# Differential attention: rotation of the heads split over ScalarE and one GpSimd multiply, softmax left undivided, output scaled on ScalarE

## The chip, the cores and the metric

The kernel runs on one core of a Trainium2 chip. The metric is the device time in microseconds of one execution, as the median of several runs. Five engines work side by side, each through its own list of instructions in order: TensorE (PE; its weight loads are PEld), VectorE (DVE), ScalarE (ACT), GpSimd (POOL) and SyncE (SP), which only starts transfers here. An instruction that waits holds up all that stand behind it on its engine.

## The reference, cut to what matters

A small network on 256 tokens of width 1024: a first block of two layers, then a second block of two. Each layer has a mixer, an attention to a memory and a feed-forward, each with a layer norm. The change touches the mixer of the first block's second layer, a differential attention with 8 heads of 2 x 64:

```python
def rope(t):
    ...
    t1, t2 = tf[..., : d // 2], tf[..., d // 2:]
    return jnp.concatenate([t1 * cos - t2 * sin, t1 * sin + t2 * cos], axis=-1).astype(t.dtype)

def block(qi):
    s = jnp.einsum('bqhcd,bkhcd->bhcqk', qi, k).astype(jnp.float32) * scale
    p = jax.nn.softmax(s, axis=-1)
    a = p[:, :, 0] - lam * p[:, :, 1]
    return jnp.einsum('bhqk,bkhe->bqhe', a.astype(v.dtype), v)

o = diff_attention(q, k, v, lam)
o = rms_norm(o, subln_g) * (1.0 - lam_init)
return o.reshape(B_, S, C_WIDTH) @ w_out
```

Queries and keys are rotated, two softmaxes of a head are subtracted with a factor `lam`, the values are weighted with the difference, and the result of each head is divided by its root mean square (with `LN_EPS` under the root).

## The kernel before, in words

All products are made in float32 precision from two parts: each weight tile `w` of 128x1024 is loaded by SyncE's queue, rounded by ScalarE to `wh` (L218), and the rest is formed by VectorE as `wl` (L219). TensorE then multiplies three times (L348, L350, L352 for products with features on the partitions; L307 to L309 in `mm3`). Four tiles can be on their way (`STAGE`), and ten pairs can lie ready (`W_SLOTS`).

There is no scheduler. The order of each engine's list is the order in which the Python code issues instructions. Heads are generators in `self.bgs`: each call of `tick` (after a projection of 128 features, `unit_group`) moves every live head to its next `yield`, and the table `PACE` says how many ticks a head rests at its points d0 to d7. So several heads are under way at once, each at another stage.

For head `h`, `odd` projects queries and keys to one PSUM bank `ps` of 128x512 (two `unit_a`), ScalarE copies it to `oqk` (L1099), and the generator `head` goes on:

- d0: GpSimd multiplies four quarters of 32 partitions by the sine table, each into the quarter beside it of `qr` (L1041); VectorE multiplies `oqk` by the cosine (L1042);
- d1: VectorE adds both to `qr` (L1044);
- d2: TensorE forms the scores of both halves of the head (L1051), VectorE their row maxima (L619, L623);
- d3: ScalarE takes the exponentials with their sums (L627, four instructions);
- d4: VectorE divides the first softmax (L631, L635 twice), takes the reciprocal of the second sum times minus `lam` (L631, L1067) and blends both (L1069 twice);
- d5: TensorE transposes the blend (L644), ScalarE copies it to `pT` (L646);
- d6: TensorE multiplies with the values (L1078), ScalarE sums the squares (L1083), VectorE adds the epsilon (L1084), GpSimd raises to the power -1/2 (L522), VectorE scales the output `oz` (L1087);
- d7: TensorE transposes it (L1091), ScalarE and VectorE split it into two parts (L295, L296).

In the middle of the stage one turn of TensorE's list is: values of head h, scores of head h+2, a half projection of head h+5, transposed output of head h, transposed blend of head h+1, the other half projection. After the last head, products of the memory's keys (`mem_fill`) take the place of the projections.

Of the kernel before, what the change touches and what calls it, by code (L numbers as in the profile page):

```python
# [15 lines left out]
S = 256  # L16
# [11 lines left out]
# ---------------------------------------------------------------- host layout  # L28


def blk_a(w):
    """[K, N] -> [N/128, 128, K] : one unit holds 128 output columns."""
    k, n = w.shape
    return w.reshape(k // 128, 128, n // 128, 128).transpose(2, 1, 0, 3).reshape(n // 128, 128, k)


def blk_v(w, ck, cols):
    """[K, N] -> [N/cols * K/128/ck, 128, ck*cols] : moving weights, ck row tiles by cols columns."""
    k, n = w.shape
    u = k // 128 // ck  # L40
    return (w.reshape(u, ck, 128, n // cols, cols).transpose(3, 0, 2, 1, 4)
            .reshape(n // cols * u, 128, ck * cols))
# [6 lines left out]
def blk_t(x):  # L49
    """[256, 1024] -> transposed [2, 128, 4*256] (two units of four feature tiles)."""  # L50
    return x.T.reshape(2, 4, 128, S).transpose(0, 2, 1, 3).reshape(2, 128, 4 * S)
# [10 lines left out]
def constants():  # L62
    i = np.arange(128)
    row, col = i[:, None], i[None, :]
    c = {}
    ident = (row == col).astype(np.float32)
    negt = np.where(row >= col, -1, 0).astype(np.float32)
    strict = (row < col).astype(np.float32)
    c["c_sq"] = np.stack([ident, negt, strict], 1).copy()
    ncn = np.zeros((128, 384), np.float32)  # L70
    ncn[:, 0:128] = np.where(col > row, -BIG, 0)
    ncn[:, 256:384] = ncn[:, 0:128]
    c["c_ncn"] = ncn
    cc = np.arange(64)
    start = np.clip(cc - 8, 0, 48)
    win = (cc[None, :] >= start[:, None]) & (cc[None, :] < start[:, None] + 16)
    na = np.where(win, 0, -BIG).astype(np.float32)
    c["c_na"] = np.tile(na[:, ::-1], (2, 6)).reshape(128, 6, 64).copy()
    inv = (np.float32(10000.0) ** (-np.arange(0, 64, 2, dtype=np.float32) / np.float32(64)))
    ang = (np.arange(S, dtype=np.float32)[:, None] * inv[None, :]).astype(np.float32)  # L80
    cos = np.tile(np.cos(ang).T.astype(np.float32), (4, 1))
    sin = np.sin(ang).T.astype(np.float32)
    sin = np.tile(np.concatenate([sin, -sin], 0), (2, 1))
    c["c_rope"] = np.stack([cos, sin], 1).copy()
    oh = np.zeros((32, 512), np.float32)
    oh[t5_buckets(), S - 1 + np.arange(S)] = 1.0
    c["c_t5"] = oh
    return c
# [79 lines left out]
# ---------------------------------------------------------------- device  # L168


class Blank:
    """Stands for every object while the order of the weights is recorded."""
# [17 lines left out]
class Stream:  # L190
    """Weights in the order of their use: loaded ahead, split into two float32r parts ahead."""
# [75 lines left out]
class Net:  # L267
# [8 lines left out]
    # ---- small helpers  # L276
# [27 lines left out]
    def mm3(self, ps, a, b, first, last):  # L304
        """ps (+)= (a0+a1)^T (b0+b1) without the product of the two low parts below float32's rounding."""
        mm = self.nc.tensor.matmul
        mm(ps, a[0], b[0], start=first, stop=False)  # L307
        mm(ps, a[0], b[1], start=False, stop=False)  # L308
        mm(ps, a[1], b[0], start=False, stop=last)  # L309
# [18 lines left out]
    def flush(self, n=99):  # L328
        """Emit up to n pieces of the layer norm that is still due."""
        while self.pending and n:  # L330
            try:
                next(self.pending[0])
            except StopIteration:
                self.pending.pop(0)
                self.ws.more(3)
            n -= 1

    # ---- projections
    def unit_group(self, units):
        """units: (ps, name, index) - 128 output features of x @ W each, feature-major, row tiles outermost."""  # L340
# [16 lines left out]
    def unit_a(self, ps, name, idx):  # L357
        """128 output features of x @ W, feature-major, into ps [128, 256]."""
        self.unit_group([(ps, name, idx)])

    def vproj(self, name, groups, evac):
        """x @ W token-major, 512 columns a group."""
# [22 lines left out]
    def vproj_first(self, name, evac):  # L385
        """The first product: each row tile as soon as it and its weights are there."""
# [16 lines left out]
    # ---- output projection, residual and layer norm  # L403
# [108 lines left out]
    def ln_r(self, t, n, c):  # L512
        """x <- c x + the columns of the output projection; their statistics."""
        nc = self.nc
        lo, hi = self.COLS[t][n]
        r = self.x[:, t, lo:hi]
        nc.vector.scalar_tensor_tensor(r, in0=r, scalar=c, in1=self.acc[t][n], op0=OP.mult, op1=OP.add)
        nc.vector.bn_stats(self.st[t][:, n, :], r)
# [27 lines left out]
    def ln_t(self, t, lo, hi):  # L546
        """Columns lo:hi of x, transposed, as two parts."""
# [7 lines left out]
    # ---- feed-forward  # L555
    def ffn(self, pre, li, c, eps, hold=6):
# [10 lines left out]
        # the first two tiles of hidden features token-major: the first tokens' part does not wait for the others  # L567
# [43 lines left out]
    # ---- softmax along the free dimension  # L611
    def softmax(self, s, src, widths, scale=1.0, norm=True):
        """s <- softmax(scale * src) for the blocks of a [128, sum(widths)]; src may be PSUM."""
# [11 lines left out]
        for i in range(n):  # L625
            w = slice(off[i], off[i] + widths[i])
            nc.scalar.activation(s[:, w], src[:, w], AF.Exp, scale=scale, bias=mx[:, i:i + 1],  # L627
                                 accum_out=sm[:, i:i + 1])
        yield
        r = self.col(n)  # L630
        nc.vector.reciprocal(r, sm)  # L631
        if norm:
            for i in range(n):
                w = slice(off[i], off[i] + widths[i])
                nc.vector.tensor_scalar(s[:, w], s[:, w], r[:, i:i + 1], None, op0=OP.mult)  # L635
        self.sm_r = r

    def transpose_p(self, s):
        """s [128 t, 2 (t), 256 s] -> [128 s, 2 (s), 256 t]."""
# [9 lines left out]
    # ---- attention to the memory  # L649
    def mem_open(self, pre, mem, kd):  # L650
        """The memory's keys and values do not depend on x: jobs that fill gaps."""
# [118 lines left out]
    # ---- layer 0 of the first block  # L770
    def even(self):
# [11 lines left out]
        def na_load(p):  # L783
            if p < 4:
                nbs[p] = [self.k2([128, 6, 64], name="bt") for _ in range(2)]
                for e, bt in enumerate(nbs[p]):
                    # rows of keys relative to the first row of the query's half, from -2; columns reversed
# [65 lines left out]
        # gates, as rows: heads of the forward direction from 0, of the backward one from 32  # L853
# [65 lines left out]
        def lstm_head(h, y):  # L919
# [13 lines left out]
            for d in range(2):  # L933
# [6 lines left out]
                # columns of E: forward (s0: t0 t1, s1: t1), backward (s0: t0, s1: t0 t1)  # L940
# [78 lines left out]
    # ---- layer 1 of the first block  # L1019
    def odd(self):  # L1020
# [4 lines left out]
        cos = rp[:, 0:1, :].to_broadcast([128, 2, S])  # L1025
# [10 lines left out]
        def head(h, qk):  # L1036
            yield from self.pause("d0")
            qr = self.k2(name="qr")
            for b in range(4):
                i, o = slice(32 * b, 32 * b + 32), slice(32 * (b ^ 1), 32 * (b ^ 1) + 32)  # L1040
                nc.gpsimd.tensor_mul(qr[o], qk[i], rp[i, 1:2, :].to_broadcast([32, 2, S]))  # L1041
            nc.vector.tensor_mul(qk, qk, cos)  # L1042
# [3 lines left out]
            ss, gs, rs = [], [], []  # L1046
            for c in range(2):
                rows = slice(64 * c, 64 * c + 64)
                ps = self.bank()
                for tt in range(2):  # L1050
# [4 lines left out]
                                 scale=0.125, norm=c == 0)  # L1055
# [3 lines left out]
            yield from self.pause("d3")  # L1059
            for g in gs:  # L1060
                next(g)
            yield from self.pause("d4")
            for g in gs:
                for _ in g:
                    pass
                rs.append(self.sm_r)
            nc.vector.tensor_scalar(rs[1], rs[1], nlam, None, op0=OP.mult)  # L1067
            for tt in range(2):
                nc.vector.scalar_tensor_tensor(ss[0][:, tt, :], in0=ss[1][:, tt, :], scalar=rs[1][:, tt:tt + 1],  # L1069
                                               in1=ss[0][:, tt, :], op0=OP.mult, op1=OP.add)  # L1070
            yield from self.pause("d5")
# [12 lines left out]
            nc.vector.tensor_scalar(q, q, 1.0 / 128, EPS, op0=OP.mult, op1=OP.add)  # L1084
            y = self.rsqrt(q, 2)
            for tt in range(2):
                nc.vector.tensor_scalar(z[:, tt, :], po[:, tt, :], y[:, tt:tt + 1], None, op0=OP.mult)  # L1087
# [6 lines left out]
        for h in range(8):  # L1094
# [3 lines left out]
            qk = self.k2(name="oqk")  # L1098
            nc.scalar.copy(qk, ps)  # L1099
            self.bgs.append(head(h, qk))  # L1100
# [4 lines left out]
    # ---- mixer of the second block  # L1105
    def mixer(self, l, li):
# [85 lines left out]
        # index scores  # L1192
# [47 lines left out]
        # the 64 largest scores of a row, lower index first among equals, as an additive mask  # L1240
# [20 lines left out]
        # the shared latent key / value  # L1261
# [4 lines left out]
        def latent():  # L1266
# [18 lines left out]
            # keys of each head's queries: the latent keys through its up-projection  # L1285
# [13 lines left out]
        # short convolution  # L1299
# [119 lines left out]
    def rel_table(self):  # L1419
        """Rows of rel_bias by distance, one for each head, to DRAM."""  # L1420
# [10 lines left out]
    def rel_rows(self, t, h):  # L1431
        """Bias of the causal blocks for each query, keys from the last to the first: distance i at 255 + i."""
# [28 lines left out]
    def tables(self):  # L1461
        nc, sg, nlam, lp = self.nc, self.sg, self.nlam, self.lp
        nc.vector.tensor_scalar(sg, sg, 1.0 - LAM_INIT, None, op0=OP.mult)
        # lambda, negated, on every partition
# [119 lines left out]
```

## Time and profile before

| | |
|---|---|
| median of 3 runs | 2338.8 us (2338.48 to 2339.41) |
| profiled execution, first to last instruction | 2336.7 us |
| busy: PE, PEld, DVE, ACT, POOL | 98%, 92%, 66%, 49%, 10% of the span |
| mean granted clock of TensorE | 0.993 of full |
| chain that ended last | PE 91%, DVE 3%, issue 2%, DMA 1%, POOL 1%, ACT 1% |
| the changed stage | about 480 to 612 us |

How to read it: the page gives no second time of the profiled execution besides its span; the runs were timed apart, and their median is 2.1 us longer than the span. A busy share is a mean over all stages. The chain is followed back from the last instruction, at each step to what released it. In the timeline a row is a start, a duration, the engine, the line of the kernel, the operation, what it writes and reads, a count, and in brackets the idle time before it with what ended it.

### The profile page before, as it was taken

How to read it: one execution, taken by the hardware profiler on the slowest of the kernel's cores; microseconds unless marked ns; L12 is line 12 of the kernel's file. 1: busy time of each engine (PE TensorE's matmuls, PEld its weight loads, DVE VectorE, ACT ScalarE, POOL GpSimd, SP SyncE). 2: the span in 40 equal slices, each digit the busy share in tenths (PEclk: the TensorE clock that was granted, in tenths of full speed). 3: DMA queues.
4: the chain of work that ended last, by engine and by line, in shares of the span. 5: the costliest groups of instructions: out<-in, count | busy, mean ns of one | idle time of the engine just before them, and what ended most of it. 6: DMA issues, size and time to landing. Idle time of an engine off the chain costs nothing.

```text
span 2336.7 us, 41017 instructions
## 1 busy us (share of the span) xinstructions
PE 2281.4 (98%) x16600; PEld 2142.5 (92%) x16600; DVE 1533.1 (66%) x2303; ACT 1138.5 (49%) x1816; POOL 241.5 (10%) x263
## 2 busy tenths in 40 slices
PE   7999999977999999999999999999999999999998
PEld 6889999977899999999999999999999999999998
DVE  5885665678757657656487677656656577677655
ACT  5555454344454444543844554443543745545542
POOL 0720000044100000000202100000000101200000
PEclk9999999998999999999999999999999999999999
DMA  7645476352355664754455555753764446454752
GB/s 236 155 163 172 162 243 189 122 192 88 128 189 181 216 189 137 242 182 136 163 154 165 170 184 184 235 184 126 253 189 155 145 142 182 156 193 165 249 186 74
DMA packets 118080, 407.50 MB, mean 174 GB/s; under 512 B 14169, under 2 KB 19418, under 8 KB 117890
## 3 DMA queue, kind: packets, MB, share of 16 engines
q1 hardware_dynamic: 116258, 402.00, 52.9%
q0 software_dynamic: 768, 1.57, 0.8%
q8 instruction: 130, 2.13, 0.4%
q10 hardware_dynamic: 864, 1.31, 0.2%
q14 instruction: 60, 0.49, 0.1%
HBM read 403.76 MB, written 1.06 MB: 173 GB/s over the span
## 4 chain that ended last, share of the span: by engine, by line
PE 91%; DVE 3%; issue 2%; DMA 1%; POOL 1%; ACT 1%; ACTq 0%; DVEq 0%; POOLq 0%; SPq 0%
PE ps L348 16%; PE ps L350 16%; PE ps L352 16%; PE acc L307 7%; PE acc L308 7%; PE acc L309 7%; PE ps L307 5%; PE ps L309 4%; PE ps L308 4%; PE ps L725 1%; PE ps L745 1%; PE ps L551 1%; PE ps L644 1%; POOL qr L1041 1%; DMA xq<-in_xT 1%
## 5 line engine op out<-in xcount | busy, mean ns | idle before, releaser
L219 DVE TENSOR_TENSOR wl<-w,wh 128x1024 fp32r<-128x1024 f32 x725 | 888.5, 1245 | 360.8 <-ACT wh L218 357.6
L348 PE MATMUL ps<-xT,wh 128*128 128x256 f32 x3232 | 924.2, 286 | 0.0
L350 PE MATMUL ps<-xT,wl 128*128 128x256 f32 x3232 | 916.9, 284 | 0.0
L352 PE MATMUL ps<-xT,wh 128*128 128x256 f32 x3232 | 916.4, 284 | 0.0
L218 ACT CAST wh<-w 128x1024 fp32r<-128x1024 f32 x725 | 748.2, 1050 | 234.5 <-PE ps L352 135.4
L348 PEld LDWEIGHTS ps<-xT,wh 128*128 128x128 f32 x3232 | 622.5, 193 | 10.0 <-issue 5.5
L350 PEld LDWEIGHTS ps<-xT,wl 128*128 128x128 f32 x3232 | 622.6, 193 | 0.6
L352 PEld LDWEIGHTS ps<-xT,wh 128*128 128x128 f32 x3232 | 622.3, 193 | 0.0
L307 PE MATMUL acc<-wh,ph 128*128 128x512 f32 (+1 forms) x940 | 329.2, 350 | 0.6 <-ACT ph L295 0.6
L308 PE MATMUL acc<-wl,ph 128*128 128x512 f32 (+1 forms) x940 | 327.2, 348 | 0.0
L309 PE MATMUL acc<-wh,pl 128*128 128x512 f32 (+1 forms) x940 | 325.9, 347 | 0.0
L307 PEld LDWEIGHTS acc<-wh,ph 128*128 128x128 f32 x940 | 177.9, 189 | 24.9 <-ACT ph L295 0.8
L309 PEld LDWEIGHTS acc<-wh,pl 128*128 128x128 f32 x940 | 177.5, 189 | 23.2 <-DVE pl L296 0.2
L308 PEld LDWEIGHTS acc<-wl,ph 128*128 128x128 f32 x940 | 178.0, 189 | 22.3
L522 POOL TENSOR_TENSOR col<-col,mhalf 128x1 f32<-128x1 f32 (+1 forms) x38 | 28.6, 753 | 1610.1 <-DVE col L530 1469.7
L563 ACT ACTIVATE k<-ps 128x256 f32<-128x256 f32 x120 | 46.0, 383 | 178.3 <-PE ps L352 178.3
L307 PE MATMUL ps<-wh 128*128 128x256 f32 x384 | 113.3, 295 | 0.0
L292 ACT CAST ph<-k 128x256 fp32r<-128x256 f32 x120 | 48.8, 407 | 129.7 <-DVE k L565 129.7
L564 DVE SCALAR_TENSOR_TENSOR k<-k,ps 128x256 f32<-128x256 f32 x120 | 50.4, 420 | 93.4 <-ACT k L563 93.2
L307 PE MATMUL ps<-wh,xT 128*128 128x256 f32 (+1 forms) x304 | 102.2, 336 | 8.5 <-ACT wh L218 8.4
L309 PE MATMUL ps<-wh,wl 128*128 128x256 f32 x384 | 109.3, 285 | 0.0
L308 PE MATMUL ps<-wl,wh 128*128 128x256 f32 x384 | 109.2, 284 | 0.0
(264 smaller groups left out, 2548.1 us busy)
## 6 DMA issues: line engine op xcount, KB each, us to landing
w<-in_h_g SPq DMA_DIRECT2D x160, 512.0 KB, 4.4
w<-in_h_d SPq DMA_DIRECT2D x88, 512.0 KB, 4.3
w<-in_f_g SPq DMA_DIRECT2D x80, 512.0 KB, 4.3
w<-in_m_gate SPq DMA_DIRECT2D x48, 512.0 KB, 4.2
w<-in_f_d SPq DMA_DIRECT2D x44, 512.0 KB, 4.1
gb<-in_ln_row SPq DMA_DIRECT2D x28, 512.0 KB, 6.5
w<-in_m_c SPq DMA_DIRECT2D x24, 512.0 KB, 3.3
w<-in_m_br SPq DMA_DIRECT2D x24, 512.0 KB, 3.5
```

The lines of the kernel that those rows point to most:

```text
L218: n.nc.scalar.copy(hi[:, :cols], w[:, :cols])
L219: self.due = lambda: n.nc.vector.tensor_sub(lo[:, :cols], w[:, :cols], hi[:, :cols].bitcast(F32))
L292: nc.scalar.copy(hi, src)
L307: mm(ps, a[0], b[0], start=first, stop=False)
L308: mm(ps, a[0], b[1], start=False, stop=False)
L309: mm(ps, a[1], b[0], start=False, stop=last)
L348: mm(ps, ws[i][0][:, k, :], xh[:, k, :], start=k == 0, stop=False)
L350: mm(ps, ws[i][1][:, k, :], xh[:, k, :], start=False, stop=False)
L352: mm(ps, ws[i][0][:, k, :], xl[:, k, :], start=False, stop=k == 7)
L522: self.nc.gpsimd.tensor_tensor(y, v, self.mhalf[:, :n], op=OP.pow)
L563: nc.scalar.activation(h, pg, AF.Tanh, scale=0.5)
L564: nc.vector.scalar_tensor_tensor(h, in0=h, scalar=1.0, in1=pg, op0=OP.add, op1=OP.mult)
```

## The change

ScalarE no longer copies `ps` to `oqk` whole: it copies its four quarters of 32 partitions, each to the neighbouring quarter of `qr`. GpSimd then multiplies all of `qr` by the sine in place, one instruction a head (the table's signs are exchanged for it). VectorE takes the cosine product straight from `ps`. The first softmax is not divided: with row sums s0 and s1, the blend is e0 - lam (s0 / s1) e1, which is s0 times the wanted difference; the epsilon under the root is multiplied by s0 squared, so that the root mean square takes the factor out again. The output is scaled by ScalarE. Lines behind the softmax shift by one to five, so the same instruction has another line number in the changed kernel.

```diff
-    sin = np.tile(np.concatenate([sin, -sin], 0), (2, 1))
+    sin = np.tile(np.concatenate([-sin, sin], 0), (2, 1))
...
+        self.sm_s = sm
         yield
+        if norm is None:
+            return
         r = self.col(n)
         nc.vector.reciprocal(r, sm)
...
-        def head(h, qk):
+        def head(h, qk, qr):
             yield from self.pause("d0")
-            qr = self.k2(name="qr")
-            for b in range(4):
-                i, o = slice(32 * b, 32 * b + 32), slice(32 * (b ^ 1), 32 * (b ^ 1) + 32)
-                nc.gpsimd.tensor_mul(qr[o], qk[i], rp[i, 1:2, :].to_broadcast([32, 2, S]))
-            nc.vector.tensor_mul(qk, qk, cos)
+            nc.gpsimd.tensor_mul(qr, qr, sin)
             yield from self.pause("d1")
             nc.vector.tensor_add(qr, qr, qk)
...
-                                 scale=0.125, norm=c == 0)
+                                 scale=0.125, norm=None)
...
+            sums = []
             for g in gs:
                 next(g)
+                sums.append(self.sm_s)
             yield from self.pause("d4")
-            for g in gs:
-                for _ in g:
-                    pass
-                rs.append(self.sm_r)
-            nc.vector.tensor_scalar(rs[1], rs[1], nlam, None, op0=OP.mult)
+
+            s0, r1 = sums
+            nc.vector.reciprocal(r1, r1)
+            nc.vector.scalar_tensor_tensor(r1, in0=s0, scalar=nlam, in1=r1, op0=OP.mult, op1=OP.mult)
             for tt in range(2):
-                nc.vector.scalar_tensor_tensor(ss[0][:, tt, :], in0=ss[1][:, tt, :], scalar=rs[1][:, tt:tt + 1],
+                nc.vector.scalar_tensor_tensor(ss[0][:, tt, :], in0=ss[1][:, tt, :], scalar=r1[:, tt:tt + 1],
                                                in1=ss[0][:, tt, :], op0=OP.mult, op1=OP.add)
+            e = self.col(2)
+            nc.vector.scalar_tensor_tensor(e, in0=s0, scalar=EPS, in1=s0, op0=OP.mult, op1=OP.mult)
...
-            nc.vector.tensor_scalar(q, q, 1.0 / 128, EPS, op0=OP.mult, op1=OP.add)
+            nc.vector.scalar_tensor_tensor(q, in0=q, scalar=1.0 / 128, in1=e, op0=OP.mult, op1=OP.add)
             y = self.rsqrt(q, 2)
             for tt in range(2):
-                nc.vector.tensor_scalar(z[:, tt, :], po[:, tt, :], y[:, tt:tt + 1], None, op0=OP.mult)
+                nc.scalar.activation(z[:, tt, :], po[:, tt, :], AF.Copy, scale=y[:, tt:tt + 1])
...
-            qk = self.k2(name="oqk")
-            nc.scalar.copy(qk, ps)
-            self.bgs.append(head(h, qk))
+
+            qk, qr = self.k2(name="oqk"), self.k2(name="qr")
+            for b in range(4):
+                o, i = slice(32 * b, 32 * b + 32), slice(32 * (b ^ 1), 32 * (b ^ 1) + 32)
+                nc.scalar.copy(qr[o], ps[i])
+            nc.vector.tensor_mul(qk, ps, cos)
+            self.bgs.append(head(h, qk, qr))
```

TensorE's and SyncE's lists keep their order. The lists of the other three change as follows. ScalarE before, one turn in the middle of the stage, from a weight cast to the next exponentials (`oz,col` are squares of a head's output with their sums, `ph` a part of its output, `pT` the transposed blend, `s,col` exponentials):

```order
L218 CAST wh<-w 128x1024
L1083 ACTIVATE oz,col<-ps 128x128 x2
L1099 COPY oqk<-ps 128x512
L218 CAST wh<-w 128x1024
L295 ACTIVATE ph<-ps,sg 128x256
L646 COPY pT<-ps 128x512
L627 ACTIVATE s,col<-ps,col 128x256 x4
```

The same turn of ScalarE in the changed kernel:

```order
L218 CAST wh<-w 128x1024
L1084 ACTIVATE oz,col<-ps 128x128 x2
L1088 ACTIVATE oz<-ps,col 128x128 x2
L1103 COPY qr<-ps 32x512 x4
L218 CAST wh<-w 128x1024
L295 ACTIVATE ph<-ps,sg 128x256
L648 COPY pT<-ps 128x512
L628 ACTIVATE s,col<-ps,col 128x256 x4
```

The scalings of the output (L1088), which need GpSimd's power, now stand right behind the squares, and one copy has become four, all ahead of the next cast.

VectorE before, the same turn, from the weight part to the blend (`col` are columns of sums and factors, `oz` the output of a head, `s` the exponentials of the next):

```order
L219 TENSOR_TENSOR wl<-w,wh 128x1024
L1084 TENSOR_SCALAR col<-col 128x2
L1087 TENSOR_SCALAR oz<-ps,col 128x128 x2
L631 RECIPROCAL col<-col 128x2
L635 TENSOR_SCALAR s<-s,col 128x256 x2
L631 RECIPROCAL col<-col 128x2
L1067 TENSOR_SCALAR col<-col,nlam 128x2
L1069 SCALAR_TENSOR_TENSOR s<-s,col 128x256 x2
```

VectorE in the changed kernel, the same place and on to the row maxima of the next head:

```order
L219 TENSOR_TENSOR wl<-w,wh 128x1024
L1085 SCALAR_TENSOR_TENSOR col<-col 128x2
L1065 RECIPROCAL col<-col 128x2
L1066 SCALAR_TENSOR_TENSOR col<-col,nlam 128x2
L1068 SCALAR_TENSOR_TENSOR s<-s,col 128x256 x2
L1071 SCALAR_TENSOR_TENSOR col<-col 128x2
L620 TENSOR_REDUCE col<-ps 128x2
L624 TENSOR_SCALAR col<-col 128x2
L620 TENSOR_REDUCE col<-ps 128x2
L624 TENSOR_SCALAR col<-col 128x2
L1104 TENSOR_TENSOR oqk<-ps,rope 128x512
```

Only instructions on 128x2 stand between the weight part and the blend now, and none of them waits for GpSimd; the cosine product (L1104) has moved behind the row maxima, and it waits for ScalarE's fourth copy from the same bank.

## Rows read from the trace of the kernel before

**Rows 1.** The page: the span, and the engines' busy time.

```profile
span 2336.7 us, 41017 instructions
PE 2281.4 (98%) x16600; PEld 2142.5 (92%) x16600; DVE 1533.1 (66%) x2303; ACT 1138.5 (49%) x1816; POOL 241.5 (10%) x263
```

**Rows 2.** TensorE's waits, 480 to 720 us: total, times, longest.

```profile
PE ps L644 <- DVE s L1069: 23.1, 6, 9.5
PE ps L1051 <- DVE qr L1044: 2.5, 2, 1.6
```

**Rows 3.** Windows: length; busy PE, PEld, DVE, ACT, POOL; clock, DMA share, GB/s.

```profile
511.40:520.90 9.50, 0.07 (x1) 0.00 (x0) 9.36 (x12) 3.62 (x9) 6.28 (x5) 0.63 0.40 131
...
534.30:544.50 10.20, 10.20 (x70) 9.40 (x70) 8.41 (x16) 5.41 (x16) 3.15 (x3) 0.83 0.32 104
...
579.60:588.20 8.60, 8.60 (x72) 8.09 (x71) 6.63 (x17) 5.26 (x18) 0.69 (x1) 1.00 0.28 93
```

**Rows 4.** TensorE's timeline: start, duration, instruction, idle time before it.

```profile
499.26 1.14 PE L1051 MATMUL ps<-qr 64*128 64x256 f32 x8 [1.58 <-DVE qr L1044]
...
520.95 1.08 PE L644 MATMUL ps<-sq,s 128*128 128x128 f32 x4 [9.47 <-DVE s L1069]
...
602.08 0.74 PE L644 MATMUL ps<-sq,s 128*128 128x128 f32 x4 [1.06 <-DVE s L1069]
```

**Rows 5.** The chain in order of time: start, duration, link.

```profile
525.89 0.91 PE ps L1078 x8
...
579.80 0.89 PE ps L1078 x8
...
585.05 0.45 PE ps L644 x4
588.37 0.89 PE ps L1078 x8
```

**Rows 6.** VectorE's timeline, GpSimd at work (two rows) and idle (two).

```profile
542.65 2.11 DVE L635 TENSOR_SCALAR s<-s,col 128x256 f32<-128x256 f32 x2
...
546.01 1.93 DVE L1069 SCALAR_TENSOR_TENSOR s<-s,col 128x256 f32<-128x256 f32 x2
...
584.13 0.88 DVE L1069 SCALAR_TENSOR_TENSOR s<-s,col 128x256 f32<-128x256 f32 x2
...
586.52 1.22 DVE L219 TENSOR_TENSOR wl<-w,wh 128x1024 fp32r<-128x1024 f32 x1
```

**Rows 7.** GpSimd's multiplies by their line: count, min/median/max ns, first and last start.

```profile
L1041 POOL TENSOR_TENSOR qr<-oqk,rope x32: 1252/1284/2175, 489.1 to 573.0; 32x512 f32<-32x512 f32 x32
```

**Rows 8.** GpSimd's groups by line and shape: busy us, mean ns, idle before.

```profile
L538 POOL TENSOR_TENSOR x<-x,gb 128x512 f32<-128x512 f32 x28 | 36.1, 1289 | 31.1 <-ACT x L537 31.1
```

**Rows 9.** ScalarE's timeline: a late cast, then one turn.

```profile
493.51 1.05 ACT L218 CAST wh<-w 128x1024 fp32r<-128x1024 f32 x1 [1.57 <-DMA w<-in_o_qk]
...
535.36 0.59 ACT L646 COPY pT<-ps 128x512 f32<-128x512 f32 x1 [3.71 <-PE ps L644]
535.85 0.48 ACT L627 ACTIVATE s<-ps,col 128x256 f32<-128x256 f32 x1
...
537.66 1.06 ACT L218 CAST wh<-w 128x1024 fp32r<-128x1024 f32 x1
540.24 0.28 ACT L1083 ACTIVATE oz<-ps 128x128 f32<-128x128 f32 x1 [1.52 <-PE ps L1078]
...
540.75 0.59 ACT L1099 COPY oqk<-ps 128x512 f32<-128x512 f32 x1
541.22 1.07 ACT L218 CAST wh<-w 128x1024 fp32r<-128x1024 f32 x1
544.59 0.47 ACT L295 ACTIVATE ph<-ps,sg 128x256 fp32r<-128x256 f32 x1 [2.30 <-PE ps L1091]
```

**Rows 10.** Timelines of VectorE and GpSimd: variance and power in that turn.

```profile
540.90 0.17 DVE L1084 TENSOR_SCALAR col<-col 128x2 f32<-128x2 f32 x1 [0.78 <-ACT oz L1083]
...
541.21 0.70 POOL L522 TENSOR_TENSOR col<-col,mhalf 128x2 f32<-128x2 f32 x1 [7.36 <-DVE col L1084]
```

More of the change, by code (lines that the diff above doesn't have):

```diff
@@ L628, in softmax @@
                                  accum_out=sm[:, i:i + 1])
+        self.sm_s = sm
         yield
+        if norm is None:
+            return
         r = self.col(n)
         nc.vector.reciprocal(r, sm)
[L632 to L636, printed above, removed]
+        for i in range(n):
+            w = slice(off[i], off[i] + widths[i])
+            nc.vector.tensor_scalar(s[:, w], s[:, w], r[:, i:i + 1], None, op0=OP.mult)
     def transpose_p(self, s):
@@ L1024, in odd @@
         nc.sync.dma_start(rp, self.a["c_rope"])
-        cos = rp[:, 0:1, :].to_broadcast([128, 2, S])
+        cos, sin = (rp[:, i:i + 1, :].to_broadcast([128, 2, S]) for i in range(2))
         v = {}
@@ L1045, in head @@
             yield from self.pause("d2")
-            ss, gs, rs = [], [], []
+            ss, gs = [], []
             for c in range(2):
```

## The prediction

> **What bounds the kernel now.** I read the page first, then TensorE's waits, then the stretches that they name on the timeline. TensorE is busy for 98% of the span [rows 1], so only time that TensorE loses can be won. It loses 23.1 us in six waits for the blended scores `s` of the differential attention and 2.5 us in two waits for the rotated heads `qr` [rows 2]; all eight lie in the stage that is changed. The reader should see in rows 3 that these waits cost twice: the granted clock is 0.63 in the stretch of the long wait and 0.83 in a stretch behind a shorter one, against 1.00 in the last turns, where the same work waits for nothing. The single waits are 1.58 us before the first scores, 9.47 us before the first transposes and 1.06 us near the end [rows 4]; the pair for `qr` leaves 2.5 - 1.58 = 0.94 for the other, and the six for `s` leave (23.1 - 9.47 - 1.06) / 4 = 3.14 us for each of four turns. The chain gives the pace of these turns: the first product with the values starts at 525.89 and the fifth at 579.80, four turns of 13.48 us; the sixth starts at 588.37, after 8.57 us [rows 5]. 8.57 us is thus what TensorE needs for a turn by itself.
>
> What makes the difference? On VectorE the two normalising instructions take 2.11 us while GpSimd multiplies, and the two blends behind them 1.93, against 0.88 when GpSimd is idle [rows 6]. GpSimd spends four quarter multiplies of 1.28 us on each head, as much for 32 partitions as 1.29 us for a full 128x512 tile [rows 7, 8]. In the last turns no head is left to rotate, and VectorE is quick again.
>
> **The change, part by part.** The profiled execution has a span of 2336.7 us [rows 1]; the median of the runs is 2338.8, so 2.1 us lie around it, and the sum is made on the span.
>
> GpSimd: 32 instructions of 1.28 become 8. No row shows this in-place shape; the add on 128x512 takes 1.29, and the longest quarter multiply, beside VectorE, 2.17 [rows 7, 8]. I take 1.3 a head; at 2.17 it would still fit, because VectorE needs the product only after the next weight part.
>
> VectorE, per head: gone are the two normalising instructions, a reciprocal and the scaling of the output; the cosine product reads PSUM now. New are three instructions on 128x2 (0.17 by the row for such a tile [rows 10]; bounded by 0 and by the 0.70 of GpSimd's work on such a tile). The chain from the row sums to the blended `s` becomes 3 x 0.17 + 0.88, about 1.4 us, where it was 5.3 (542.65 to the end of the blends at 547.94 [rows 6]).
>
> ScalarE, per head: one copy of 0.59, of which 0.47 pass before the next instruction starts [rows 9], becomes four on 32 partitions, and two scalings of the output are added. No row shows a copy to other partitions. Lower bound: a quarter of the lanes for a quarter of the price, 0.12; upper bound: 2.17, the longest 32x512 row of any engine [rows 7]. I take 0.47, as the same 512 elements pass along each lane, and as GpSimd's price did not fall with the partitions. The Trainium skill (ScalarE: Activation LUTs, "What ACT_TABLE_LOAD costs") has the time of an ACTIVATE set by the elements of a lane, 186 ns + 0.833 ns each with an overlap of 93 ns: estimated 0.52 us a copy here. By it the loop below would be 0.2 us longer and the result 0.3 us later; the trace's 0.47 for the full copy agrees roughly, and no row shows the quarter.
>
> The two scalings (about 0.4 together, like the squares at 540.24 without their sums) stand in ScalarE's order directly behind the squares and wait for GpSimd's power. Behind them are queued the four copies, a weight cast, the parts of the output, the copy of the transposed scores, the exponentials and the next cast. That closes a loop through ScalarE. From the start of the cast ahead of the squares: cast 1.06, then VectorE's weight part 1.22 [rows 6] (it is in front of the variance), variance 0.17 and power 0.70 with their hand-overs 0.25 [rows 10]: 3.4; scalings 0.4; copies 4 x 0.47 = 1.88; cast 0.95; output part 0.45; transposed copy 0.49; exponentials 1.81 [rows 9]. Sum 9.4 us a turn. This exceeds TensorE's 8.57: ScalarE is what comes late next, by 0.8 us a turn.
>
> The start. Today a cast behind the first head's copy waits for its DMA until 493.51 [rows 9]; the three extra copies fit into that wait. From the second head on they shift the casts by 1.4 us a head. Following the two engines' orders with the prices above, head 0 is rotated by about 495, its row maxima are ready at about 502 and `s` at 507.5. TensorE gets to the first transposes at 520.95 - 9.47 - 2.52 = 508.96. So all three waits go, with a margin of 1.5 us; but the fourth head's multiply (about 507 to 508) can fall on the first blend, which disturbed costs 0.5 more each, so I subtract 0.4. The Trainium skill (GPSIMD Engine Reference, "Key points") says that GpSimd contends with VectorE's instructions that have two SBUF inputs or use the two-port mode; the blend has two, and rows 6 agree. Without that rule nothing is subtracted.
>
> The sum:
> - first part: 2.52 + 9.47, and the low clock behind it: transposes to values take 525.89 - 520.95 = 4.94 there [rows 4, 5], 3.32 at full clock (588.37 - 585.05 [rows 5]), less 0.2 as the chain picks different matmuls: 1.4. Together 13.4;
> - four turns, 53.9 today. ScalarE enters about 1.7 us ahead of need, so two turns stay at 8.57, one takes 8.9, one 9.4: 35.4. Saved 18.5;
> - fifth turn: no copies, but ScalarE is still behind: 9.15 for 8.57, lost 0.6;
> - the wait of 1.06 near the end goes, as VectorE's chain is over 1 us shorter: 1.06;
> - the disturbed blend: lost 0.4.
>
> Saved 13.4 + 18.5 - 0.6 + 1.06 - 0.4 = 32.0. Span 2336.7 - 32.0 = 2304.7, with 2.1 around it **2306.8 us**.
>
> Costed at nothing: the loads. They move 93 to 104 GB/s in these turns and 131 at most in the long wait [rows 3]; at 9 us a turn the same two weight parts of 0.52 MB need 117. What follows the stage is TensorE's own and is only moved earlier. No activation table is loaded in the stage, before or after.
>
> **The rivals.**
> 1. ScalarE does not bind: the copies cost 0.12 to 0.3. The loop falls to 8.0 to 8.7, and every turn takes 8.57: 13.4 + 53.9 - 34.3 + 1.06 = 34.1, time 2304.7. For it: only a quarter of the lanes is read. Against: the price on GpSimd does not follow the partitions [rows 7, 8].
> 2. Part of the loss remains. A copy of 0.7 makes a turn 10.3: the last three turns lose 0.9 each, and the first `s` comes 16 x 0.23 = 3.7 us later, a wait of some 2.2 us. That costs 2.7 + 2.2 + 1 for the clock: saved 26, time 2312.7. A multiply that still held GpSimd for 5.2 us a head, so that the change did not do what it says, would delay the add and the weight part ahead of the variance, a turn of about 10.6: saved some 25, 2314. Against that: the full tile at 1.29 [rows 8].
> 3. Slower: the copies that shift partitions are slow, as 32-partition work is on GpSimd. Sixteen of them stand ahead of the first `s`, sixteen more in the four turns. The margins take about 1.5 + 1.7 us; beyond them each 0.1 us a copy costs 3.2 us. The gain of 32 is used up where a copy takes about 0.47 + 35 / 32 = 1.6 us. At 2.17 the time is 2338.8 - 32.0 + 54.4 - 3.2 = 2358. For it: no row excludes it. Against: on ScalarE a full 128x512 copy costs 0.59 whatever it is for.
>
> **How the numbers follow.** The forecast 0.60, rival 1 0.15, rival 2 0.21, rival 3 0.04. What this kernel's measurement can tell from no change is about 0.2%, 4.7 us. All of the forecast and of rivals 1 and 2 are faster by more; rival 3 gives 0.02 slower, and 0.02 for a copy price at which gain and loss meet. Faster 0.95, same 0.02, slower 0.03 (0.01 for what I have not seen). Range: down to rival 1 with 1.7 to spare, 2303; up past rival 2, 2315.
>
> **What would show it.** Right: the quarter copies at 0.5 to 0.6 each; one multiply of 1.3 a head; the normalising instructions gone and the blends at 0.45 each; no wait of TensorE over 1 us in the stage, small waits of 0.3 to 0.9 for ScalarE's scaled output; turns of 8.6 to 9.5 and a clock of 1.00; the sixth product with the values near 556. Wrong: a wait before the first transposes that is still several us, a clock below 0.95 in the turns, copies over 0.7, or turns of 10 us and more.

## The result, and the profile after

The changed kernel takes 2308.0 us (median of 4 runs, 2305.7 to 2310.0) against 2338.8 for the kernel before (2338.5 to 2339.4), 0.9869 of its time (95% interval 0.9855 to 0.9882). The forecast was 2306.8, in a range of 2303 to 2315. The profiled execution is the longest of the four: 2310.0, with a span of 2308.3.

The page first. TensorE's busy time is the same to 1%, the span is shorter, and the weight loads and VectorE lose little; GpSimd's busy time is down by 40 us and ScalarE's up by 18.

```profile
span 2308.3 us, 40983 instructions
...
PE 2277.5 (99%) x16600; PEld 2139.0 (93%) x16600; DVE 1498.5 (65%) x2271; ACT 1156.3 (50%) x1856; POOL 201.9 (9%) x239
```

TensorE's waits over the whole span (engine and line waited for, total us, times, longest). The waits for `s` and for `qr` of [rows 2] are gone. The first two rows lie outside the changed stage and are there before as well (8.4 and 7.5). Three waits for ScalarE's copy of the transposed scores are new, 2.6 us in all.

```profile
PE ps L307 <- ACT wh L218: 9.4, 2, 7.0
PE ps L551 <- POOL x L538: 7.5, 12, 2.0
PE ps L1079 <- ACT pT L648: 2.6, 3, 1.1
```

The first two stretches of time of [rows 3], with the same columns; the work in them is further on now. The granted clock is 1.00 where it was 0.63 and 0.83.

```profile
511.40:520.90 9.50, 9.50 (x80) 9.02 (x80) 7.20 (x16) 7.88 (x22) 2.00 (x2) 1.00 0.33 112
534.30:544.50 10.20, 9.41 (x74) 8.44 (x73) 7.36 (x17) 8.24 (x22) 1.99 (x2) 1.00 0.31 104
```

TensorE's timeline, to be read against [rows 4, 5]: the first scores, the first transposes, six products with the values and the eighth. Neither the first scores nor the first transposes wait. Five turns take 8.55, 9.41, 9.94, 10.30 and 9.07 us; the brackets show what the later ones wait for.

```profile
498.29 1.14 PE L1049 MATMUL ps<-qr 64*128 64x256 f32 x8
...
509.36 0.60 PE L646 MATMUL ps<-sq,s 128*128 128x128 f32 x4
...
512.68 1.05 PE L1079 MATMUL ps<-ov,pT 128*128 128x128 f32 x8
...
521.23 1.05 PE L1079 MATMUL ps<-ov,pT 128*128 128x128 f32 x8
...
530.64 1.16 PE L1079 MATMUL ps<-ov,pT 128*128 128x128 f32 x8 [0.71 <-ACT pT L648]
...
540.58 1.16 PE L1079 MATMUL ps<-ov,pT 128*128 128x128 f32 x8 [0.79 <-ACT pT L648]
...
550.88 1.16 PE L1079 MATMUL ps<-ov,pT 128*128 128x128 f32 x8 [1.07 <-ACT pT L648]
...
559.95 1.05 PE L1079 MATMUL ps<-ov,pT 128*128 128x128 f32 x8
...
575.55 1.05 PE L1079 MATMUL ps<-ov,pT 128*128 128x128 f32 x8
```

The chain of waits shows what holds these turns. This is one round of it (start, us, engine, line): from one cast on ScalarE through VectorE's weight part and GpSimd's power back to ScalarE, and there through scalings, copies, cast, output part, transposed copy and exponentials to the next cast, 532.42 - 522.39 = 10.03 us later; the rounds before and behind it take 9.97 and 9.95. No instruction of TensorE is in it, and TensorE by itself needs 8.55 a turn.

```profile
522.39 0.94 ACT wh L218
523.36 1.23 DVE wl L219
524.81 0.70 POOL col L522
525.53 0.63 ACT oz L1088 x2
526.18 0.58 ACT qr L1103
...
528.56 1.05 ACT wh L218
529.63 0.47 ACT ph L295
530.11 0.47 ACT pT L648
530.58 1.84 ACT s L628 x8
532.42 0.94 ACT wh L218
```

VectorE is quick again. Two rows of its timeline, and below them two of GpSimd's. The blends of the first head take 0.88, as when GpSimd is idle [rows 6]. The first row shows how the two engines meet: 128x2 elements, 0.17 us elsewhere, take 0.97 and end at 502.66, just behind the multiply, which ends at 502.63.

```profile
501.69 0.97 DVE L624 TENSOR_SCALAR col<-col 128x2 f32<-128x2 f32 x1
...
507.28 0.88 DVE L1068 SCALAR_TENSOR_TENSOR s<-s,col 128x256 f32<-128x256 f32 x2
```

```profile
501.33 1.30 POOL L1040 TENSOR_TENSOR qr<-qr,rope 128x512 f32<-128x512 f32 x1 [3.10 <-ACT qr L1103]
508.08 1.32 POOL L1040 TENSOR_TENSOR qr<-qr,rope 128x512 f32<-128x512 f32 x1 [5.44 <-ACT qr L1103]
```

### The profile page after: what moved, and what is told of

It is laid out like the page before. It is cut to its first block, busy times and chain, and to the rows that moved or that the text cites. A ratio compares the mean times of both kernels' runs of the same rounds, so it can differ in the third digit from the quotient of the medians.

```text
span 2308.3 us, 40983 instructions
## 1 busy us (share of the span) xinstructions
PE 2277.5 (99%) x16600; PEld 2139.0 (93%) x16600; DVE 1498.5 (65%) x2271; ACT 1156.3 (50%) x1856; POOL 201.9 (9%) x239
## 3 DMA queue, kind: packets, MB, share of 16 engines
HBM read 403.76 MB, written 1.06 MB: 175 GB/s over the span
## 4 chain that ended last, share of the span: by engine, by line
PE 95%; ACT 2%; DVE 2%; DMA 1%; POOL 0%; issue 0%; ACTq 0%; DVEq 0%; POOLq 0%
PE ps L348 17%; PE ps L350 16%; PE ps L352 16%; PE acc L307 7%; PE acc L308 7%; PE acc L309 7%; PE ps L307 5%; PE ps L309 5%; PE ps L308 5%; PE ps L551 1%; PE ps L727 1%; PE ps L747 1%; DMA xq<-in_xT 1%; PE ps L646 1%; DVE x L536 0%; PE ps L1145 0%
```

## The experiments

Theory: two things were wrong before, GpSimd's 5.2 us a head beside VectorE and the length of VectorE's chain behind the softmax, and the first is the larger; what is left of the loss is the loop through ScalarE. Rivals: the gain comes from the normalising instructions that are gone; the turns are held by something else than ScalarE's order. In brackets stand the ratio to the kernel before, which ran on the same chip and took 2337.6 to 2338.8 us (medians), and its 95% interval. The edits are told in short, with loops on one line; the first two are against the kernel before, the others against the changed kernel. The changed kernel itself took 2308.0.

### One multiply, without the undivided softmax

```diff
+ for b in range(4): nc.scalar.copy(qr[o], ps[i])
- for b in range(4): nc.gpsimd.tensor_mul(qr[o], qk[i], sin quarter)
+ nc.gpsimd.tensor_mul(qr, qr, sin)
  (cosine product straight from ps, as in the changed kernel)
  (softmax divided, VectorE scales, as before)
```

> The kernel before with the rotation of the change alone: four ScalarE copies and one GpSimd multiply of a head; the softmax stays divided and VectorE scales the output. Theory A (the gain comes from GpSimd being busy 1.3 instead of 5.2 us a head, so that VectorE is no longer disturbed): row sums to blended s take 0.17 x 3 + 2 x 0.46 + 0.88 = 2.3 us instead of 5.3, the long wait of 9.47 falls under 2 us, turns of 8.6 to 9.5; at least 80% of the gain, 2315 us or less. Rival B (the gain comes from the normalising instructions that are gone): at most 40% of the gain, 2326 us or more. Rival C (either alone takes enough out of the chain): this and the undivided softmax alone both come to 2315 or less.

Measured 2310.0 us (0.9874, 0.9857 to 0.9890): 28.8 of 30.8 us, 93% of the gain. Theory A holds. Later turns take 9.6 to 10.1, over the 8.6 to 9.5 expected, and wait for `s` again, 0.7 to 1.1 each: VectorE's timeline of one turn has the divided softmax in the way, and its 128x2 instruction is held until GpSimd's multiply (527.40, 1.46 long) is over.

```profile
527.10 0.62 DVE L636 TENSOR_SCALAR s<-s,col 128x256 f32<-128x256 f32 x2
527.63 0.16 DVE L632 RECIPROCAL col<-col 128x2 f32<-128x2 f32 x1
527.82 1.07 DVE L1064 TENSOR_SCALAR col<-col,nlam 128x2 f32<-128x2 f32 x1
528.92 0.88 DVE L1066 SCALAR_TENSOR_TENSOR s<-s,col 128x256 f32<-128x256 f32 x2
```

### The undivided softmax and ScalarE's scaling, without the one multiply

```diff
  (one ScalarE copy, four quarter multiplies on GpSimd, as before)
- normalise first softmax; blend; VectorE scales
+ blend undivided with r1 = s0 * nlam / s1; ScalarE scales
```

> The kernel before with the undivided softmax and ScalarE's scaling alone: the rotation stays four quarter multiplies on GpSimd. Theory A (GpSimd's time is the cause): the blends still take 1.9 for 0.88 beside the multiplies, the add of the rotated halves still waits for 5.2 us of GpSimd; at most half of the gain, 2323 us or more. Rival B (the normalising instructions): at least 80% of the gain, 2315 us or less. Rival C (either alone is enough): 2315 or less here and in the one-multiply run.

Measured 2322.8 us (0.9932, 0.9917 to 0.9947): 52% of the gain, just over the half that A allowed and far from rival B's 80%. The two shares add to 145%, so part of the gain is had by either. What stays shows on TensorE, GpSimd and VectorE at the first head: GpSimd works through twelve quarters in 22.74 us, the two blends take 2.95 for 0.88, and the first transposes wait 6.81.

```profile
516.75 0.66 PE L646 MATMUL ps<-sq,s 128*128 128x128 f32 x2 [6.81 <-DVE s L1072]
```

```profile
487.53 22.74 POOL L1043 TENSOR_TENSOR qr<-oqk,rope 32x512 f32<-32x512 f32 x12 [29.35 <-issue]
```

```profile
515.06 2.95 DVE L1072 SCALAR_TENSOR_TENSOR s<-s,col 128x256 f32<-128x256 f32 x2
```

In the later turns the blends take 0.88 again, which A did not expect. There GpSimd's four quarters act by another way: VectorE's cosine product waits for them, and the weight part, the variance, GpSimd's power and ScalarE's scaling stand behind it. TensorE waits 5.3 us in four waits for the scaled output, and the third and fourth turns take 11.02 and 12.51. The undivided softmax with VectorE's scaling was not run, so its own share stays open.

```profile
545.02 0.69 DVE L1044 TENSOR_TENSOR oqk<-oqk,rope 128x512 f32<-128x512 f32 x1 [3.46 <-POOL qr L1043]
```

```profile
548.93 0.59 PE L1096 MATMUL ps<-sq,oz 128*128 128x128 f32 x2 [2.10 <-ACT oz L1092]
```

### The changed kernel with quarter multiplies

```diff
- nc.gpsimd.tensor_mul(qr, qr, sin)
+ for b in range(4): nc.gpsimd.tensor_mul(qr[o], qr[o], sin[o])
```

> The changed kernel with GpSimd's one multiply of a head cut into four of 32 partitions, some 5.2 us a head again. Theory (GpSimd's time is the main cause, and the shorter chain behind the softmax only softens it): the blends take 1.9 for 0.88 again, the add waits for the multiplies, 2314 us or more, towards the 2322.8 of the undivided softmax alone. Rival (ScalarE's loop holds the turns whatever GpSimd does): 2308 to 2310 us.

Measured 2320.5 us (0.9923, 0.9906 to 0.9939): cutting the one multiply into four costs 12.6 us of the changed kernel's time. The loss stands at the first head: 8.29 us before the first transposes, at a clock of 0.65, and 0.62 in the stretch behind. Ahead of them VectorE's adds of rotated halves wait up to 2.56 for quarters, and the first head's blends take 2.96; in the turns the blends take 0.88, not the 1.9 expected. The turns hardly change (8.55, 9.71, 10.28, 10.57, 9.07), so they are held by ScalarE, as the rival said of them alone.

```profile
516.49 0.66 PE L646 MATMUL ps<-sq,s 128*128 128x128 f32 x2 [8.29 <-DVE s L1070]
```

```profile
508.00:516.50 8.50, 0.21 (x3) 0.04 (x1) 8.43 (x9) 5.46 (x12) 6.79 (x6) 0.65 0.44 148
516.50:522.00 5.50, 4.85 (x27) 4.45 (x28) 5.25 (x10) 3.36 (x10) 0.97 (x1) 0.62 0.00 0
```

### One copy in place of four

```diff
- for b in range(4): nc.scalar.copy(qr[o], ps[i])
+ nc.scalar.copy(qr, ps)
```

> The changed kernel with one copy of the whole tile in place of the four shifted ones (the halves are not swapped, so the heads are rotated wrongly). If the loop through ScalarE holds the turns: 10.0 - 3 x 0.59 = 8.2 us, below TensorE's 8.55, so every turn 8.55 and 2303.5 us, as with the scaling on VectorE. If the wait for the power holds them whatever the copies: turns stay at 9.4 to 10.3, 2308 us.

Measured 2304.0 us (2303.1 to 2304.6; 0.9850, 0.9836 to 0.9865). Every turn takes 8.54: from the first to the sixth product 42.72 us, where the changed kernel takes 47.27. The 4.55 us are the 4.5 expected, and they are what the loop through ScalarE costs. The halves are not swapped here, so this is a test and no version to keep. ScalarE's timeline shows the copy of the full tile:

```profile
516.01 0.59 ACT L1101 COPY qr<-ps 128x512 f32<-128x512 f32 x1
516.48 1.07 ACT L218 CAST wh<-w 128x1024 fp32r<-128x1024 f32 x1
```

### The scaling back on VectorE

```diff
- nc.scalar.activation(z[:, tt, :], po[:, tt, :], AF.Copy, scale=y[:, tt:tt + 1])
+ nc.vector.tensor_scalar(z[:, tt, :], po[:, tt, :], y[:, tt:tt + 1], None, op0=OP.mult)
```

> The changed kernel with the scaling of the output back on VectorE. If the loop through ScalarE (10.0 us a turn, 1.1 to 1.7 of it a wait for GpSimd's power and 0.63 the scalings) is what holds the turns: without these it is 7.7, below TensorE's 8.55, the turns fall from 9.41, 9.94, 10.30 and 9.07 to 8.55, 4.5 us are saved, 2303.5 us. Rival: VectorE now waits for the power with the weight part queued behind it and becomes the bound: no gain or a loss, 2308 to 2312 us.

Measured 2307.2 us (2306.0 to 2308.2), 0.8 less than the changed kernel, within the spread: the forecast of 2303.5 missed. ScalarE is no longer the bound, but TensorE waits 1.9 us in five waits for `s`. VectorE (first fence) idles 0.87 for the power and then comes to its blends as GpSimd (second fence) starts the next multiply; they take 1.89 for 0.88.

```profile
523.41 0.61 DVE L1088 TENSOR_SCALAR oz<-ps,col 128x128 f32<-128x128 f32 x2 [0.87 <-POOL col L522]
...
524.38 1.89 DVE L1068 SCALAR_TENSOR_TENSOR s<-s,col 128x256 f32<-128x256 f32 x2
```

```profile
524.31 1.28 POOL L1040 TENSOR_TENSOR qr<-qr,rope 128x512 f32<-128x512 f32 x1 [0.93 <-ACT qr L1103]
```

### The scaling one step later, on ScalarE and on VectorE

```diff
  y = self.rsqrt(q, 2)
+ yield
  for tt in range(2):
      (scale z by y: on ScalarE in the first run, on VectorE in the second)
```

> The changed kernel with ScalarE's two scalings of a head issued one step later (half a turn, behind the copies and a cast), and the pair of transposes behind them as well. If ScalarE's wait for the power (1.1 to 1.7 us a turn) closes the loop that holds the turns: the copies fill it, the loop falls from 10.0 to about 8.4, turns of 8.55, sixth product with the values near 555.5 instead of 559.95, 2303.5 to 2304.5 us. Rival: what waits for the scaled output (the transposes, its parts) comes half a turn later and TensorE waits there or near the end of the stage: 2306 to 2309 us.

> The changed kernel with the scaling on VectorE and one step later. In the run with the scaling on VectorE the blends stood behind the wait for the power and met GpSimd's multiply (1.89 us for 0.88). If that collision is why that run won only 0.75 us: here the blends stand ahead of the multiply and take 0.88, no wait for s is left, turns of 8.55, 2303.5 to 2304.5 us. Rival: VectorE is simply full (some 8 of 8.55 us a turn): waits for s of 0.3 to 0.5 stay, 2306 to 2307.5 us.

Measured 2303.5 us (2302.4 to 2304.3; 0.9849, 0.9835 to 0.9864) and 2302.4 us (2300.9 to 2304.5; 0.9846, 0.9831 to 0.9860). Both leave nothing of the computation out; with the next one they are the quickest such versions. On ScalarE the copies and a cast now stand where it waited for the power:

```profile
521.28 0.27 ACT L1084 ACTIVATE oz<-ps 128x128 f32<-128x128 f32 x1
521.66 2.35 ACT L1104 COPY qr<-ps 32x512 f32<-32x512 f32 x4
524.03 1.05 ACT L218 CAST wh<-w 128x1024 fp32r<-128x1024 f32 x1
525.11 0.63 ACT L1089 ACTIVATE oz<-ps,col 128x128 f32<-128x128 f32 x2
525.63 0.59 ACT L648 COPY pT<-ps 128x512 f32<-128x512 f32 x1
```

In the same kernel the products come at 511.36 and, five turns of 8.56 later, at 554.14; near the end TensorE waits 0.56, as in the changed kernel, so the late reader that the rival expected doesn't show. With the scaling on VectorE the blends stand ahead of the multiply and take 0.88 again, and no wait for `s` is left:

```profile
523.18 0.88 DVE L1068 SCALAR_TENSOR_TENSOR s<-s,col 128x256 f32<-128x256 f32 x2
```

So the idle 0.87 and the collision behind it, which both go here, took the gain of the run with the scaling on VectorE, and not a full VectorE: the work on it is the same. The multiply now holds an instruction on 128x2 elements (1.28 for 0.17), and TensorE waits for nothing there.

### The multiply on VectorE as well

```diff
  (on top of ScalarE's scaling one step later)
- nc.gpsimd.tensor_mul(qr, qr, sin)
+ nc.vector.tensor_mul(qr, qr, sin)
```

> The changed kernel with ScalarE's scalings one step later and the multiply of a head on VectorE: GpSimd keeps only the power. If what counts is that GpSimd's long instructions are away from VectorE: 0.68 us more on VectorE a head, some 7.8 of 8.55 us a turn, still fits; turns of 8.55, 2303 to 2304 us, as with the multiply on GpSimd. Rival: VectorE is full with it, waits for s or for the rotated heads come back: 2306 us or more.

Measured 2302.5 us (2300.9 to 2305.3; 0.9851, 0.9836 to 0.9865), turns of 8.55. GpSimd is not needed for the multiply: VectorE takes half the time for it. Whether this or the two versions above are quicker by a microsecond can't be told from these runs.

```profile
L1040 DVE TENSOR_TENSOR qr<-qr,rope x8: 683/686/689, 492.3 to 543.4; 128x512 f32<-128x512 f32 x8
```

### The price of a copy: not shifted, and made twice

```diff
- nc.scalar.copy(qr[o], ps[i])
+ nc.scalar.copy(qr[o], ps[o])
```

> The changed kernel with the four copies of 32 partitions left on their own partitions (the halves are not swapped). If moving to other partitions costs the overlap with the neighbours: 0.47 us from start to start, 1.9 for four, turns shorter by 0.5. If any copy of a quarter pays it: 0.59 from start to start, 2.35 for four, as in the changed kernel.

A single run, 2307.7 us. Four copies take 2.33 where the shifted ones take 2.35, and the turns stay at 8.55 to 10.14. What a quarter costs is not the move to other partitions.

```profile
527.16 2.33 ACT L1103 COPY qr<-ps 32x512 f32<-32x512 f32 x4
529.52 1.05 ACT L218 CAST wh<-w 128x1024 fp32r<-128x1024 f32 x1
```

```diff
- for b in range(4):
+ for b in (0, 1, 2, 3, 0, 1, 2, 3):
```

> The changed kernel with each of the four copies made twice: 2.35 us more of ScalarE a head, as if a copy cost 1.18. By the slope of the rival that forecast a loss (16 copies ahead of the first s, 16 in the four turns, each 0.1 us a copy 3.2 us once the margins are gone, and they are gone at 0.59): 32 x 0.59 = 18.9 us more, 2327 us, a wait of several us before the first transposes and turns of 12.3. Rival: ScalarE has idle time ahead of the first s that absorbs its 9.4 us: turns of 12.3 alone, 2308 + 4.5 x 2.35 = 2318.5 us or less.

Measured 2327.4 us (2325.3 to 2329.5; 0.9954, 0.9938 to 0.9971), the 2327 of the slope. Both parts of it are there: TensorE waits 4.44 before the first transposes, at a clock of 0.67 from 508.2 to 518.6, and the middle turns take 12.4 to 12.7. From the first product to the eighth 75.4 us pass instead of 62.9, and the first comes 5.9 later: 18.4 together. The sum is that of the slope and its halves are not: it put 9.4 in each, and 12.5 and 5.9 came. The turn behind the four long ones takes 11.47 with TensorE busy throughout, at a clock of 0.73, so part of the agreement is luck.

```profile
512.66 1.08 PE L646 MATMUL ps<-sq,s 128*128 128x128 f32 x4 [4.44 <-DVE s L1068]
...
541.82 1.60 PE L1079 MATMUL ps<-ov,pT 128*128 128x128 f32 x8 [3.23 <-ACT pT L648]
```

```profile
566.92:578.39 11.47, 11.47 (x71) 10.44 (x71) 6.76 (x16) 8.40 (x29) 0.69 (x1) 0.73 0.39 139
```

## Why the prediction was right, and where its sizes were off

**Where the time is.** It lay where the prediction had it, in the waits for `qr` and `s` and in the low clock behind them, and the cause it named, GpSimd beside VectorE, is the main one: the one multiply alone brings 93%, the undivided softmax with ScalarE's scaling 52%. Taken out of the changed kernel, the one multiply costs 12.6 us; the undivided softmax and ScalarE's scaling cost 2.0, which lies within the spread of the runs.

**First part.** Forecast 13.4, less 0.4 for a disturbed blend. The first product comes at 512.68 instead of 525.73: 13.05. That it fits to 0.05 is luck: no blend was disturbed, and the profiled execution reached its first scores 0.6 later (498.29, against 499.26 - 1.58 = 497.68 without the wait before). Counted from there 13.66 are saved. The head start of 1.5 us was real and measured 1.2 (`s` ready at 508.16, transposes at 509.36). The fourth multiply started at 508.08, as the blends ended, and held a 128x2 instruction instead, which nobody waited for. GpSimd's 1.3 a head was right (1.294 to 1.323 us).

**The lock.** In these rows VectorE is not slowed by GpSimd, it stands until GpSimd's instruction has ended: 502.66 against 502.63 above, and 528.89 against 528.86 in the run with one multiply. Not every instruction is held: the reciprocal of that run takes 0.16 in the middle of the same multiply (527.63). The Trainium skill (SBUF — State Buffer, "SBUF: two separate sides") calls the pair of ports that GpSimd shares with VectorE's instructions that have two SBUF inputs or use a two-port mode an exclusive lock, held for a whole instruction; the trace agrees in the two ends 0.03 us behind GpSimd's. With it the forecast could have said why four quarters back to back do more harm than one multiply of the same length as a single quarter: each blend meets another quarter (2.95 for both).

**Four turns: the step that was mis-sized.** The prediction closed the right loop through ScalarE, forecast 9.4 us, measured 10.03. Two of its terms were too small: four copies 1.88, measured 2.38 with the gaps (0.577 each, and the next starts only when one has ended, while a full copy gives 0.12 back to its neighbour); two scalings 0.4, measured 0.65. Cast, output part, transposed copy and exponentials make up another 0.15, and cast to power with the hand-overs were 0.25 shorter than allowed. The loop was thus 1.5 us longer than TensorE's turn, not 0.8; four turns took 38.20 instead of 35.4, and 15.7 were saved, not 18.5. So the sixth product came at 559.95, not near 556. The prediction named turns of 10 us as a sign against it: the fourth took 10.30, with 0.37 for a copy of the memory's keys (L673) that stands in ScalarE's list there, and the longest wait was 1.07. The waits came at the transposed copy, further down the same loop, not at the scaled output. The Trainium skill (ScalarE: Activation LUTs, "What ACT_TABLE_LOAD costs") gave an estimate of 0.52 a copy, with its overlap taken off; without the overlap the estimate by its 186 ns + 0.833 ns an element is 0.61, nearer to the 0.577 here.

**The rest.** The fifth turn lost 0.5 (forecast 0.6). From the sixth product to the eighth 15.60 us pass instead of 17.24: the wait of 1.06 is gone, and 0.6 more. Some 0.4 of that goes with the wait: in the run with the scaling on VectorE, too, turns with a wait of 0.38 for `s` take 9.33 for 8.55. No run here explains the other 0.2, nor why a wait for `s` costs more than its length. Together 13.05 + 15.7 - 0.5 + 1.64 = 29.9 by the eighth product, against 32.0. The profiled span saved only 28.4. The other 1.5 lie behind the stage: from the eighth product to the end 1732.75 us pass against 1731.25 before, and that stretch varied from 1729.7 to 1732.8 over all twelve profiles, with nothing changed in it. So the forecast of the median, 1.2 us too low, came out closer than its turns: the profiled execution is the longest of four, and scatter of this size hides part of the 2.1 us by which the stage fell short. Of the 2.1 us that the prediction put around the span, 1.7 are there in each run; the other 0.4 was scatter between two runs.

**The rivals.** Rival 3's slope (3.2 us for each 0.1 us a copy) was tested with doubled copies and held in the sum. For rival 1, a ScalarE that does not bind, the one-copy run stands: 2304.0, forecast 2304.7. Rival 2's second half, a multiply that still held GpSimd, was put at 2314 by longer turns; the run gave 2320.5, and by another way: the turns stayed, and the first head's wait came back, since the quarters of three heads stand one behind the other there.

## What to carry to other kernels

Where GpSimd's instructions hold up VectorE's, count how long they run, in one piece and back to back, and what VectorE has queued just then; a multiply on 32 partitions cost what one on 128 did (1.28 and 1.30 us). When work moves to an engine that is half idle, close the loop through its list with the trace's start-to-start times, not with its busy share: ScalarE was busy 8.2 of 10.2 us and still held every turn, because an instruction waited for another engine in front of independent work. Issuing that one a step later brought the 4.5 us back.

## What the runs showed of the hardware that was not expected

- ScalarE's copies on 32 partitions of 512 elements take 0.577 us, as long as the full tile's 0.59, and follow each other without overlap, shifted to other partitions or not (2.35 and 2.33 for four); a full copy lets the next instruction start 0.47 after its own start.
- VectorE's row maxima and cosine product, which read PSUM, kept their 0.68 and 0.69 us beside GpSimd's multiplies; so did reciprocals on 128x2 elements (0.16). Blends, weight parts and `TENSOR_SCALAR` from SBUF did not, down to 128x2 elements (0.17 became 0.97).
- Waits of 0.7 to 1.1 us a turn left the granted clock at 1.00; with waits of 2.0 to 3.5 us a turn (copies twice) it was 0.86 to 1.00 by turn and 0.73 in the turn behind them, and with 3.1 before the change 0.83 [rows 3].
